# Two gates and the first weights of a convolution, taken step by step in another order

## The chip, the cores and the metric

The kernel runs on one core of one Trainium2 chip. A core has TensorE (matrix products, in the profile PE, its weight loads PEld), VectorE (DVE), ScalarE (ACT), GpSimd (POOL) and SyncE (SP), whose queue starts the transfers from device memory. Each engine runs its own instructions strictly in the order of its own list; between engines there are semaphores. The metric is the device time of one execution in microseconds, and lower is better.

## The reference, cut to what matters

An encoder trunk of two layers runs over two sequences of 512 and 256 tokens (768 columns together), with 1024 features (eight blocks of 128 rows) in float32. Layer 0 mixes tokens by attention within a window, layer 1 by a gated convolution of width 3. After each mixer comes an MLP and then a gated embedding. The places that matter here are the gated embedding that ends layer 0 and the start of the convolution:

```
h = rms_norm(x, norm_ple[0])
x = x + (p[0] @ ple_w_proj[0]) * sigmoid(h @ ple_w_gate[0])
h = rms_norm(x, norm_mix[1])
b_gate, c_gate, u = split(h @ conv_w_in)
z = c_gate * u
```

## The kernel before, in words

Activations lie transposed: a block `x(m)` is 128 features by 768 tokens. Every float32 operand is split in two parts, a high part (`whi`, `zhi`, `vhi` for weights, `xs` and `t` for inputs) written by ScalarE and a low part (`wlo`, `zlo`, `vlo`), which is the operand less its high part, written by VectorE. A product takes high by high, high by low and low by high on TensorE. Weights arrive as `wraw`, 128x1024 each, in three buffers; a fourth fetch waits until the low part of the first has been taken.

`ple` computes the gated embedding for the eight blocks in the order 0, 4, 1, 5, 2, 6, 3, 7 (`PAIRED`). For one block TensorE makes the gate product (two banks of 384 columns). VectorE multiplies it by the reciprocal root `r` (`gt<-gate`, L1206, for the last block L1259), ScalarE takes the sigmoid (L1207, L1260), VectorE multiplies by the projected embedding `pr` and adds to `x` (L1208 and L1210, L1266 and L1267). Then the block is made ready for the next norm `n3` (`plain_block`): ScalarE writes `xs<-x` times the gain, VectorE its low part (L304 and L305 for the first four blocks, L309 and L310 for the others), ScalarE squares the block (L195, L1273) and VectorE adds the square to `acc` (L196, L1280).

The convolution's products, save the first, use a scheme of seven smaller products on halves of 384 columns. They need sums of blocks: ScalarE copies two blocks (`q`, L326), VectorE makes four sums (`t13`, L345 and L346, and `t42`, L350 and L351), and ScalarE and VectorE split the two results (`high`, L355, and `low`, L361). The weights need sums as well (`sums32`, L409 and L410; `sums14`, L414 and L415), and their parts are split at L434 (high) and L445 (low), in groups called direct, second, s32, s14 and w22.

`conv_weights(0, 0, True)`, named `c`, is the first pair of weight arrays of the convolution. It is used as it comes, in 96 matmuls (`plain`, L1499: 48 for output `c1` with `zhi` and `zlo`, 48 for `c2` with `whi` and `wlo`, the last group of six of each 48 being that of block 7). `conv_weights(1, 0)`, named `v`, is the second pair, for the first of the eleven products of seven (`seven`). Between them stands the norm: `acc` is split into `ah` and `al` (L83, L84), four matmuls with ones give the sum of squares `ss` (L235), and `rstd_steps` makes the reciprocal root of it in three steps. `logs` is `v<-ss` on VectorE (L252), and `ln<-ss`, an exponential and a square on ScalarE (L254, L255, L256); `newton` is L260 and `result` L267 on VectorE. The logarithm needs another table than the sigmoid, and `table()` loads it (L216). `squares` then squares the root into `r2` on ScalarE (L1510), and `first(0)`, `first(1)` multiply `c1` and `c2` by it (L1516).

Inside `seven` these steps wait in a list, `pend`, and `late(n)` takes the next `n` at fixed places. For the first product of seven all four single banks `a`, `c`, `b` and `d` are of tag A. It runs as twelve matmuls each, L466: `a` (w11), then the copy `c<-a` (L1533), `b` (s3), `a` again (s2), the copy `d<-a` (L1547), `c` (w12), `a` (s1), `d` (w22), `a` (s4). `low<-a,p` (L1472) must have read `a` after s1 before s4 writes it again.

The order of ScalarE, TensorE and VectorE in this stretch is the order in which the code is written, since it stands in `tc.manual_schedule` blocks. The transfers' order on SyncE follows from the scheduler.

Of the kernel before, what the change touches and what calls it, by code (L numbers as in the profile page):

```python
# [13 lines left out]
AF = mybir.ActivationFunctionType  # L14
ALU = mybir.AluOpType
# [5 lines left out]
KB = D // P  # L21
SEQS = (512, 256)
T = sum(SEQS)
# [24 lines left out]
def trunk_kernel(ctx: ExitStack, tc: tile.TileContext, a: dict, out: bass.AP):  # L48
    nc = tc.nc
    act, dve, pe = nc.scalar, nc.vector, nc.tensor  # L50
# [13 lines left out]
    def gain(i, m):  # L64
        return vec[:, i * KB + m : i * KB + m + 1]
# [26 lines left out]
    def weight(src, n, raw=None, tag="w"):  # L92

        m = CH if src is None else src.shape[1]
        if raw is None:
            raw = fetch(src)
        pool, bufs = (wp, 2) if tag == "w" else (more, 1)
        hi, lo = (pool.tile([P, CH], F32R, tag=f"{tag}{p}", name=f"{tag}{p}", bufs=bufs) for p in ("hi", "lo"))
        split(hi[:, :m], lo[:, :m], raw[:, :m])
        return blocks(hi[:, :m], n), blocks(lo[:, :m], n)  # L100
# [15 lines left out]
    def both(name="mm", tag=None):  # L116

        return [t[:, :H] for t in fresh(name, 2, tag)]
# [29 lines left out]
    def slot(i, name, dt=F32R, n=T):  # L148

        return (slots if i < 32 else more).tile([P, n], dt, tag=f"S{i}", name=name)  # L150

    def big(name, dt=F32):

        nonlocal turn
        if more is None:
            return tmp.tile([P, T], dt, tag="t", name=name)
        turn += 1
        return tmp.tile([P, T], dt, tag=f"q{turn % 6}", name=name, bufs=1)
# [12 lines left out]
    class Norm:  # L171
# [9 lines left out]
        def block(self, m, xb):  # L181
            g = gain(self.i, m)
            hi, lo = (slot(self.places[8 * p + m], f"xs_{self.name}") for p in range(2))
            self.xs[0].append(hi[:])
            self.xs[1].append(lo[:])
            act.activation(hi[:], xb, AF.Copy, scale=g)
            dve.scalar_tensor_tensor(lo[:], xb, g, hi[:].bitcast(F32), ALU.mult, ALU.subtract)
            self.square(m, xb)
# [91 lines left out]
    class Norm7(Norm):  # L280
# [9 lines left out]
        def place(self):  # L290
            return slot(self.free.pop(0), "xs7")
# [40 lines left out]
    class Sums:  # L332
# [30 lines left out]
        def steps(self):  # L363
            return [
                self.t13,
                lambda: self.high(0),
                self.t42,
                lambda: self.high(1),
                lambda: self.low(0),
                lambda: self.low(1),  # L370
            ]
# [97 lines left out]
    pj = [dram.tile([KB, P, T], F32, name=f"pj{l}") for l in range(2)]  # L469
# [353 lines left out]
    def x(m, o=0, n=T):  # L823
        return pairs[m // 2][:, m % 2, o : o + n]
# [8 lines left out]
    PAIRED = [m + i for m in range(KB // 2) for i in (0, KB // 2)]  # L833
# [356 lines left out]
    def gate(w, xs, o, n):  # L1190
        ts = terms_of(w, [[t[:, o : o + n] for t in p] for p in xs])
        if n == T:
            gp = both("gate")
            group2(gp, ts)
            return pieces(gp)
        gp = fresh("gate")
        group(gp, ts, n)
        return [(gp[:, :n], 0, n)]

    def gated(l, m, gp, r, o, n, nxt, places):  # L1200

        pr = places(m) if callable(places) else slot(places[m % 3], "pr", F32)
        nc.sync.dma_start(pr[:, :n], pj[l][m, :, o : o + n])
        t = big("gt")
        for ps, i, e in gp:
            dve.tensor_tensor(t[:, i:e], ps, r[:, o + i : o + e], ALU.mult)  # L1206
        nxt.gated = act.activation(t[:, :n], t[:, :n], AF.Sigmoid).ins  # L1207
        dve.tensor_tensor(t[:, :n], pr[:, :n], t[:, :n], ALU.mult)  # L1208
        xb = x(m, o, n)
        dve.tensor_tensor(xb, xb, t[:, :n], ALU.add)  # L1210
        return xb

    def ple(norm, nxt):

        def place(m):
            return more.tile([P, CH], F32, tag=("sum0", "sum1", "zhi")[PAIRED.index(m) % 3], name="pr", bufs=1)

        def product(m, w):
            return gate(w, norm.xs, 0, T)

        def weights(i):
            return weight(a["gate"][0, PAIRED[i]], KB)

        def block(i, gp):
            m = PAIRED[i]
            nxt.block(m, gated(0, m, gp, r, 0, T, nxt, place))

        r = None
        for i in range(5):
            gp = product(PAIRED[i], weights(i))  # L1230
            r = norm.rstd(psum) if r is None else r
            block(i, gp)
            if i in (1, 3):
                weave(nxt.combine(i // 2))
        gp = product(PAIRED[5], weights(5))
        with tc.manual_schedule(engines={ET.Activation, ET.PE, ET.DVE}):
            w6 = weights(6)
            block(5, gp)
            w7 = weights(7)
            g6 = product(PAIRED[6], w6)  # L1240
            c = conv_weights(0, 0, True)
            sums = nxt.copied(2, 6)
            sums.t13()
            sums.t42()
            g7 = product(PAIRED[7], w7)
            block(6, g6)
            c.split("direct")
            sums.high(0)
            sums.high(1)
            sums.low(0)  # L1250
            sums.low(1)
            c.high("second")
            v = conv_weights(1, 0)
            m = KB - 1
            pr = place(m)
            nc.sync.dma_start(pr[:, :T], pj[0][m])
            t = big("gt")
            for ps, o, e in g7:
                dve.tensor_tensor(t[:, o:e], ps, r[:, o:e], ALU.mult)  # L1259
            nxt.gated = act.activation(t[:], t[:], AF.Sigmoid).ins  # L1260
            nxt.last = nxt.gated
            nxt.table()
            c.low("second")
            sq = big("sq")
            nxt.copied(m - KB // 2)
            dve.tensor_tensor(t[:], pr[:, :T], t[:], ALU.mult)  # L1266
            dve.tensor_tensor(x(m), x(m), t[:], ALU.add)  # L1267
            nxt.plain_block(m, x(m))
            sums = nxt.copied(m)
            v.sums32()  # L1270
            sums.t13()
            sums.high(0)
            act.activation(sq[:], x(m), AF.Square)  # L1273
            v.high("direct")
            sums.t42()
            v.low("direct")
            sums.high(1)
            sums.low(0)
            sums.low(1)
            dve.tensor_tensor(nxt.acc, nxt.acc, sq[:], ALU.add)  # L1280
            v.high("s32")
            parts = nxt.acc_parts()
            v.sums14()
            v.low("s32")
        return c, v, parts

    def last_ple(norm, full, rest, prs, ys, finals):
# [107 lines left out]
    def conv_weights(kind, p, plain=False):  # L1395
        f = (KB, 2 * KB, 0)[kind] + p
        return Weights7(a["w_in"][f], a["w_in"][f + KB // 2], plain)

    def mixer_conv(norm, w, v, norm_parts, held, finals, places, outs):
# [11 lines left out]
        pend, after, kept, done = [], [], {}, {}  # L1411
# [77 lines left out]
        def plain(w):  # L1489

            ps = [both(f"c{i + 1}", "BC"[i]) for i in range(2)]
            for i in range(2):
                for k in range(KB):
                    m, h = PAIRED[k] % (KB // 2), PAIRED[k] // (KB // 2)
                    c = slice(P * m, P * m + P)
                    hi, lo = w.w[f"w{i + 1}{h + 1}"]
                    for j, (wt, part) in enumerate(((hi, 0), (hi, 1), (lo, 0))):
                        for o in range(2):
                            pe.matmul(  # L1499
                                ps[i][o],  # L1500
                                lhsT=wt[:, c],
                                rhs=xs[f"x{h + 1}{1 + o}"][m][part],
                                start=k == 0 and j == 0,
                                stop=k == KB - 1 and j == 2,
                            )
            logs, newton, result = norm.rstd_steps(psum, norm.sum_squares(psum, parts=norm_parts, tag="A"))

            def squares():
                result()
                act.activation(r2[:], norm.r, AF.Square)  # L1510

            def first(i):
                kept["c", i] = big(f"c{i + 1}")
                for o in range(2):
                    c = slice(H * o, H * o + H)
                    dve.scalar_tensor_tensor(  # L1516
                        kept["c", i][:, c], ps[i][o], 1.0 - 2 * i, r2[:, c], ALU.mult, ALU.mult
                    )

            pend.extend([logs, newton, squares, lambda: first(0), lambda: first(1)])  # L1520

        a_out = a["w_out"]

# [89 lines left out]
    behind, product, w0 = second_inputs(xs0[24:])  # L1613
    w = [weight(a["w_o0"][2], 4)] * 2
    w2 = weight(a["w_o2"], 2, tag="z")
    for i, m in enumerate(PAIRED):
        if i == 1:
            w += [weight(a["w_o0"][3], 4)] * 2
        ps = both()
# [103 lines left out]
```

## Time and profile before

| what | value |
|---|---|
| time, median of 3 runs | 1702.33 us (1701.73 to 1704.52) |
| time of the profiled execution | 1702.36 us |
| its span, first to last instruction | 1700.6 us |
| TensorE busy over the span | 97% |
| VectorE, ScalarE busy | 83%, 53% |
| TensorE busy in 865 to 906 us | 36.27 of 41.00 us |
| TensorE busy in 906 to 1060 us | 153.69 of 154.00 us |

Times in the profile are microseconds from the start of the span. A row of the timeline gives the start, the length, the engine, the line, the operation with its output and inputs, the shape, how many like it were merged, and in brackets how long the engine had sat idle before it and for whose result. One engine's next instruction can start before the one ahead has ended, so the distance between starts is shorter than an instruction's length.

### The profile page before, as it was taken

To read this page: it belongs to the slowest core of one execution; us is meant where nothing else is said; L and a number is where in the kernel's file an instruction comes from. 1 tells how busy PE (TensorE), PEld (TensorE's weight loads), DVE (VectorE), ACT (ScalarE), POOL (GpSimd) and SP (SyncE) were. 2 spreads that over 40 slices of the span, in tenths; PEclk is the share of its full clock that TensorE was granted. 3 is DMA by queue.
4 is the path that set the end of the run, shared out by engine and by line. 5 is a ranking of instruction groups with operands and counts; after the bars stand their busy time and mean duration, and the time that the engine had idled before them with its cause. 6 is when DMAs were issued, how large, how long until landed. Compare 5 with 4: busy or idle time off the path is not lost.

```text
span 1700.6 us, 24086 instructions
## 1 busy us (share of the span) xinstructions
PE 1653.7 (97%) x9410; PEld 1592.2 (94%) x9410; DVE 1415.1 (83%) x2304; ACT 907.5 (53%) x1451; POOL 1.0 (0%) x12
## 2 busy tenths in 40 slices
PE   8999999989999999999999999999999999999996
PEld 7887788989999999999999999999999999999986
DVE  6588888889999989987888877858999999998776
ACT  6367756754455455544654334545445445554544
POOL 0000000000000000000000000000000000000000
PEclk9999999999999999999999999999999999999998
DMA  8654322211122211221212212211122211222222
GB/s 262 193 135 121 106 81 81 87 50 67 71 76 74 74 70 68 74 99 66 100 60 75 74 63 76 76 61 50 62 75 74 74 67 72 75 74 86 82 76 93
DMA packets 47843, 144.58 MB, mean 85 GB/s; under 512 B 6081, under 2 KB 10689, under 8 KB 47729
## 3 DMA queue, kind: packets, MB, share of 16 engines
q1 hardware_dynamic: 45168, 139.89, 24.2%
q10 hardware_dynamic: 2560, 3.15, 0.7%
q8 instruction: 74, 1.21, 0.3%
q14 instruction: 41, 0.33, 0.1%
HBM read 123.10 MB, written 10.48 MB: 79 GB/s over the span
## 4 chain that ended last, share of the span: by engine, by line
PE 59%; DVE 29%; ACT 8%; issue 3%; DMA 0%; DVEq 0%; ACTq 0%; SPq 0%
PE a L466 17%; PE mm L129 9%; PE mm L138 8%; PE b L466 4%; PE gate L138 4%; PE B L466 3%; PE C L466 3%; DVE t L361 3%; DVE wlo L445 3%; DVE y L938 3%; DVE zlo L445 2%; DVE act L394 1%; PE d L466 1%; ACT y L941 1%; DVE sum L410 1%
## 5 line engine op out<-in xcount | busy, mean ns | idle before, releaser
L434 ACT ACTIVATE whi<-sum 128x1024 fp32r<-128x1024 f32 x67 | 70.5, 1052 | 146.9 <-PE a L466 146.9
L941 ACT ACTIVATE y<-y 128x768 f32<-128x768 f32 x64 | 53.7, 840 | 144.6 <-DVE y L938 144.5
L466 PE MATMUL a<-xs,whi 128*128 128x384 f32 x624 | 123.4, 340 | 4.2 <-ACT whi L434 3.4
L466 PEld LDWEIGHTS a<-xs,whi 128*128 128x128 f32 x624 | 111.2, 189 | 4.9 <-ACT whi L434 3.7
L466 PE MATMUL a<-t,zhi 128*128 128x384 f32 x536 | 109.9, 338 | 3.4 <-ACT c L1054 3.1
L466 PE MATMUL b<-t,zhi 128*128 128x384 f32 x536 | 109.4, 338 | 0.5 <-ACT ln L254 0.5
L466 PE MATMUL a<-t,whi 128*128 128x384 f32 x536 | 108.8, 336 | 0.9 <-ACT d L1547 0.9
L466 PEld LDWEIGHTS a<-t,zhi 128*128 128x128 f32 x536 | 94.9, 188 | 4.3 <-ACT c L1054 3.8
L466 PE MATMUL a<-act,whi 128*128 128x384 f32 x448 | 96.5, 337 | 0.0
L466 PEld LDWEIGHTS b<-t,zhi 128*128 128x128 f32 x536 | 95.4, 189 | 0.9 <-ACT ln L254 0.9
L466 PEld LDWEIGHTS a<-t,whi 128*128 128x128 f32 x536 | 94.8, 188 | 1.2 <-ACT d L1547 1.2
L445 DVE TENSOR_TENSOR wlo<-wraw,whi 128x1024 fp32r<-128x1024 f32 x72 | 87.7, 1217 | 6.8 <-ACT whi L434 6.8
L445 DVE TENSOR_TENSOR wlo<-sum,whi 128x1024 fp32r<-128x1024 f32 x67 | 81.9, 1222 | 10.2 <-ACT whi L434 10.2
L1110 DVE TENSOR_TENSOR x<-x,a 128x384 f32<-128x384 f32 x112 | 60.7, 552 | 33.9 <-PE a L466 33.6
L434 ACT ACTIVATE zhi<-sum 128x1024 fp32r<-128x1024 f32 x67 | 71.0, 1060 | 22.3 <-DVE sum L410 22.2
L138 PE MATMUL mm<-xs_mix,whi 128*128 128x512 f32 (+1 forms) x320 | 82.9, 342 | 0.0
L434 ACT ACTIVATE whi<-wraw 128x1024 fp32r<-128x1024 f32 x72 | 75.7, 1052 | 11.6 <-PE C L466 6.1
L445 DVE TENSOR_TENSOR zlo<-sum,zhi 128x1024 fp32r<-128x1024 f32 x67 | 81.6, 1217 | 0.0
L466 PEld LDWEIGHTS a<-act,whi 128*128 128x128 f32 x448 | 79.9, 188 | 0.0
L355 ACT ACTIVATE t<-y 128x768 fp32r<-128x768 f32 x56 | 47.1, 842 | 41.2 <-DVE y L346 30.7
L83 ACT ACTIVATE whi<-wraw 128x1024 fp32r<-128x1024 f32 (+2 forms) x49 | 50.0, 1019 | 34.4 <-PE mm L129 13.9
L466 PE MATMUL a<-xs,wlo 128*128 128x384 f32 x312 | 67.7, 339 | 0.1
(316 smaller groups left out, 4488.0 us busy)
## 6 DMA issues: line engine op xcount, KB each, us to landing
wraw<-in_up SPq DMA_DIRECT2D x64, 512.0 KB, 3.5
wraw<-in_down SPq DMA_DIRECT2D x64, 512.0 KB, 3.5
wraw<-in_w_in SPq DMA_DIRECT2D x24, 512.0 KB, 3.5
wraw<-in_gate SPq DMA_DIRECT2D x16, 512.0 KB, 3.5
pj<-pjs SPq DMA_DIRECT2D x16, 384.0 KB, 3.3
wraw<-in_w_q SPq DMA_DIRECT2D x8, 512.0 KB, 4.8
wraw<-in_w_out SPq DMA_DIRECT2D x8, 512.0 KB, 3.5
x_in<-in_x SPq DMA_DIRECT2D x8, 384.0 KB, 7.6
```

Source lines behind the costliest of these rows:

```text
L83: first = act.activation(hi, src, AF.Copy)
L129: pe.matmul(t, lhsT=w, rhs=x[:, o:e], start=first and i == 0 and j == 0, stop=last and i == n - 1 and j == 2)
L138: pe.matmul(ps[:, o:e], lhsT=w, rhs=x[:, o:e], start=i == 0 and j == 0, stop=i == n - 1 and j == 2,)
L355: act.activation(t[0][:], (self.q1, self.q2)[i][:], AF.Copy)
L361: dve.tensor_tensor(lo[:], (self.q1, self.q2)[i][:], hi[:].bitcast(F32), ALU.subtract)
L394: dve.tensor_tensor(lo[:], self.q2[:], hi[:].bitcast(F32), ALU.subtract)
L434: act.activation(hi[:], src, AF.Copy)
L445: dve.tensor_tensor(lo[:], src, hi[:].bitcast(F32), ALU.subtract)
L466: pe.matmul(ps, lhsT=a, rhs=b, start=start and i == 0, stop=i == len(terms) - 1, skip_group_check=True)
L938: dve.scalar_tensor_tensor(t[:, o:e], src, 0.0, r[:, o:e], op, ALU.mult)
L941: act.activation(t[:], t[:], AF.Square)
L1110: dve.tensor_tensor(t[:, o : o + H], t[:, o : o + H], f, op)
```

## The change

The helper `block` of `ple` becomes `steps`, which gives the four steps of a gate apart: `times`, `sigmoid`, `added` and the making ready of the block. For the first six gates they are called one after the other as before. For the last two, blocks 3 and 7, the splits of the weights `c` and `v` and of the sums are written in between. The table load goes behind the square of block 7, the low part of s32 ahead of `al`, and in the convolution the square of the root (`r2`) goes from one step of `pend` to the next one, behind the copy `d<-a`. No instruction is added or taken away on any of the engines.

```
-            block(5, gp)
+            for step in steps(5, gp):
+                step()
             w7 = weights(7)
-            g6 = product(PAIRED[6], w6)
+            gp = product(PAIRED[6], w6)
             c = conv_weights(0, 0, True)
             sums = nxt.copied(2, 6)
             sums.t13()
             sums.t42()
-            g7 = product(PAIRED[7], w7)
-            block(6, g6)
-            c.split("direct")
+            times, sigmoid, added, block = steps(6, gp)
+            gp = product(PAIRED[7], w7)
+            c.high("direct")
+            times()
+            c.low("direct")
+            sigmoid()
+            c.high("second")
+            added()
+            c.low("second")
             sums.high(0)
+            block()
+            sums.high(1)
+            v = conv_weights(1, 0)
+            times, sigmoid, added, block = steps(7, gp)
+            m = KB - 1
+            sums.low(0)
+            nxt.copied(m - KB // 2)
+            times()
+            sigmoid()
+            sums.low(1)
+            v.sums32()
+            added()
+            nxt.plain_block(m, x(m))
+            sums = nxt.copied(m)
+            v.high("direct")
+            v.low("direct")
+            sums.t13()
+            sums.high(0)
+            v.high("s32")
+            sums.t42()
             sums.high(1)
             sums.low(0)
             sums.low(1)
-            c.high("second")
...
+            sq = big("sq")
+            act.activation(sq[:], x(m), AF.Square)
             nxt.last = nxt.gated
             nxt.table()
...
             dve.tensor_tensor(nxt.acc, nxt.acc, sq[:], ALU.add)
-            v.high("s32")
+            v.low("s32")
             parts = nxt.acc_parts()
             v.sums14()
-            v.low("s32")
...
             def squares():
-                result()
                 act.activation(r2[:], norm.r, AF.Square)
+                first(0)
...
-            pend.extend([logs, newton, squares, lambda: first(0), lambda: first(1)])
+            pend.extend([logs, newton, result, squares, lambda: first(1)])
```

ScalarE's list from the copies of blocks 2 and 6 (`q`, the first row) to the last sigmoid, before:

```order
L326 ACTIVATE q<-x,vec 128x768 x2
L1207 ACTIVATE gt<-gt 128x768
L304 ACTIVATE xs_8878<-x,vec 128x384
L304 ACTIVATE x_8879<-x,vec 128x384
L195 ACTIVATE sq<-x 128x768
L434 ACTIVATE zhi<-wraw 128x1024
L355 ACTIVATE t_8891<-q 128x768
L355 ACTIVATE t_8894<-q 128x768
L434 ACTIVATE whi<-wraw 128x1024
L1260 ACTIVATE gt<-gt 128x768
L216 ACT_TABLE_LOAD
```

The same stretch now:

```order
L326 ACTIVATE q<-x,vec 128x768 x2
L434 ACTIVATE zhi<-wraw 128x1024
L1235 ACTIVATE gt<-gt 128x768
L434 ACTIVATE whi<-wraw 128x1024
L355 ACTIVATE t_8886<-q 128x768
L304 ACTIVATE xs_8889<-x,vec 128x384
L304 ACTIVATE x_8890<-x,vec 128x384
L195 ACTIVATE sq<-x 128x768
L355 ACTIVATE t_8898<-q 128x768
L326 ACTIVATE q<-x,vec 128x768
L1235 ACTIVATE gt<-gt 128x768
```

The high part `zhi` of the convolution's first weights now stands ahead of the sigmoid of block 3, `whi` right behind it, and the table load has left this stretch.

VectorE's list from the product's multiplication by `r` for block 7 (`gt<-gate`) to the low part of that block's input (`xs_8922`), before:

```order
L1259 TENSOR_TENSOR gt<-gate,rstd_ple_8336 128x384 x2
L445 TENSOR_TENSOR wlo<-wraw,whi 128x1024
L1266 TENSOR_TENSOR gt<-pr,gt 128x768
L1267 TENSOR_TENSOR x<-x,gt 128x768
L310 SCALAR_TENSOR_TENSOR xs_8922<-x,vec,xs_8921 128x768
L409 TENSOR_TENSOR sum<-wraw 128x512
L410 TENSOR_TENSOR sum<-sum,wraw 128x512
```

And now:

```order
L1232 TENSOR_TENSOR gt<-gate,rstd_ple_8336 128x384 x2
L361 TENSOR_TENSOR t_8899<-q,t_8898 128x768
L409 TENSOR_TENSOR sum<-wraw 128x512
L410 TENSOR_TENSOR sum<-sum,wraw 128x512
L1238 TENSOR_TENSOR gt<-pr,gt 128x768
L1239 TENSOR_TENSOR x<-x,gt 128x768
L310 SCALAR_TENSOR_TENSOR xs_8922<-x,vec,xs_8921 128x768
L445 TENSOR_TENSOR wlo<-wraw,whi 128x1024
```

The sums of the second pair of weights moved ahead of the last addition to `x`, and `wlo` of the first pair has gone to the gate of block 3; the `wlo` that ends the second list is that of the second pair.

ScalarE's list from the copies of block 7 to the first part of the norm's sum (`ah`), as one piece of the difference:

```order
 L326 ACTIVATE q<-x,vec 128x768
-L355 ACTIVATE t_8931<-q 128x768
-L1273 ACTIVATE sq<-x 128x768
-L434 ACTIVATE whi<-wraw 128x1024
+L434 ACTIVATE whi<-wraw 128x1024
+L355 ACTIVATE t_8933<-q 128x768
+L434 ACTIVATE zhi<-sum 128x1024
 L355 ACTIVATE t_8941<-q 128x768
-L434 ACTIVATE zhi<-sum 128x1024
+L1296 ACTIVATE sq<-x 128x768
+L216 ACT_TABLE_LOAD
 L83 ACTIVATE ah<-acc_mix_8258 128x768
```

The square of block 7 and the table load now stand last ahead of `ah`.

More of the change, by code (lines that the diff above doesn't have):

```diff
@@ L1222, in weights, with steps, times, sigmoid @@
             return weight(a["gate"][0, PAIRED[i]], KB)
-        def block(i, gp):
+        def steps(i, gp):
             m = PAIRED[i]
-            nxt.block(m, gated(0, m, gp, r, 0, T, nxt, place))
+            pr = place(m)
+            nc.sync.dma_start(pr[:, :T], pj[0][m])
+            t = big("gt")
+            def times():
+                for ps, o, e in gp:
+                    dve.tensor_tensor(t[:, o:e], ps, r[:, o:e], ALU.mult)
+            def sigmoid():
+                nxt.gated = act.activation(t[:], t[:], AF.Sigmoid).ins
+            def added():
+                dve.tensor_tensor(t[:], pr[:, :T], t[:], ALU.mult)
+                dve.tensor_tensor(x(m), x(m), t[:], ALU.add)
+            return times, sigmoid, added, lambda: nxt.block(m, x(m))
         r = None
@@ L1231, in ple @@
             r = norm.rstd(psum) if r is None else r
-            block(i, gp)
+            for step in steps(i, gp):
+                step()
             if i in (1, 3):
@@ L1237, in ple @@
             w6 = weights(6)
-            block(5, gp)
+            for step in steps(5, gp):
+                step()
             w7 = weights(7)
-            g6 = product(PAIRED[6], w6)
+            gp = product(PAIRED[6], w6)
             c = conv_weights(0, 0, True)
@@ L1251, in ple @@
             sums.low(1)
-            c.high("second")
[L1253 to L1260, printed above, removed]
+            sq = big("sq")
+            act.activation(sq[:], x(m), AF.Square)
             nxt.last = nxt.gated
             nxt.table()
[L1263 to L1279, printed above, removed]
             dve.tensor_tensor(nxt.acc, nxt.acc, sq[:], ALU.add)
-            v.high("s32")
+            v.low("s32")
             parts = nxt.acc_parts()
             v.sums14()
-            v.low("s32")
         return c, v, parts
```

## The prediction, on record before the changed kernel ran

> **What bounds the kernel now.** First the page's span, then the waits of TensorE from 800 to 925 us, then its timeline around the change, then the stage windows. The waits:
>
> ```profile
> span 1700.6 us, 24086 instructions
> ...
> PE c L1499 <- ACT zhi L434: 1.1, 1, 1.1
> PE a L466 <- ACT d L1547: 0.9, 1, 0.9
> PE ss L235 <- DVE al L84: 0.5, 1, 0.5
> PE b L466 <- ACT ln L254: 0.5, 1, 0.5
> ...
> PE c L1499 <- DVE xs L310: 0.4, 1, 0.4
> ...
> ```
>
> The reader is to see that TensorE's waits of this stretch lie at the seam between the last gate and the convolution's first products, and behind both other engines: new weights (`zhi`), the last block (`xs`), the norm's sum (`al`), its logarithm (`ln`) and a copy (`d`). Next TensorE's rows there:
>
> ```profile
> 872.60 0.52 PE L129 MATMUL gate<-xs_ple,wlo 128*128 128x384 f32 x2
> ...
> 883.98 0.33 PE L1499 MATMUL c<-xs,whi 128*128 128x384 f32 x1
> ...
> 891.97 0.51 PE L1499 MATMUL c<-xs,wlo 128*128 128x384 f32 x2
> ...
> 894.62 1.56 PE L466 MATMUL a<-xs,whi 128*128 128x384 f32 x8
> ...
> 905.42 1.66 PE L466 MATMUL a<-t,whi 128*128 128x384 f32 x8 [0.92 <-ACT d L1547]
> ...
> 909.72 1.57 PE L466 MATMUL a<-xs,whi 128*128 128x384 f32 x8
> ```
>
> From 883.98 to 891.97 stand 46 starts without a wait, so a matmul costs 7.99/46 = 0.174 us. The gate's last two start at 872.60, so the convolution is due at 872.95. Up to 905.42 stand 96 + 4 + 4x12 = 148 matmuls, 25.7 us, but 32.47 pass: 6.75 us are lost, and 0.1 more behind the last wait, since the distance after a wait is longer (8 matmuls in 1.66 there, 1.57 at 909.72). So 6.9 us is all that can be had. What is won stays won if nothing new waits later:
>
> ```profile
> 906.00:1060.00 154.00, 153.69 (x877) 152.74 (x876) 122.06 (x173) 59.35 (x82) 0.00 (x0) 1.00 0.19 70
> ```
>
> TensorE (first pair) is busy 153.69 of 154.00 there, VectorE (third) 122.06, so VectorE has room to follow an earlier TensorE.
>
> **The change part by part.** Nothing is added or removed; the sum is over starts. I walk the new lists with the old durations and the old distances between starts. The clock is that of the old trace, and nothing ahead of 865.4 moves.
>
> ```profile
> 863.64 1.75 ACT L326 ACTIVATE q<-x,vec 128x768 f32<-128x768 f32 x2
> 868.39 0.85 ACT L1207 ACTIVATE gt<-gt 128x768 f32<-128x768 f32 x1 [3.00 <-DVE gt L1206]
> ...
> 878.95 1.28 ACT L216 ACT_TABLE_LOAD   x1
> 880.24 0.94 ACT L326 ACTIVATE q<-x,vec 128x768 f32<-128x768 f32 x1
> ...
> 886.43 0.83 ACT L1273 ACTIVATE sq<-x 128x768 f32<-128x768 f32 x1
> 887.17 1.04 ACT L434 ACTIVATE whi<-wraw 128x1024 fp32r<-128x1024 f32 x1
> 888.11 0.83 ACT L355 ACTIVATE t<-q 128x768 fp32r<-128x768 f32 x1
> ```
>
> ```profile
> 867.35 1.01 DVE L1206 TENSOR_TENSOR gt<-gate,rstd_ple 128x384 f32<-128x384 f32 x2
> ...
> 875.30 1.82 DVE L361 TENSOR_TENSOR t<-q,t 128x768 fp32r<-128x768 f32 x2
> 877.03 1.01 DVE L1259 TENSOR_TENSOR gt<-gate,rstd_ple 128x384 f32<-128x384 f32 x2
> 877.97 1.21 DVE L445 TENSOR_TENSOR wlo<-wraw,whi 128x1024 fp32r<-128x1024 f32 x1
> 879.10 0.95 DVE L1266 TENSOR_TENSOR gt<-pr,gt 128x768 f32<-128x768 f32 x1
> 880.08 0.96 DVE L1267 TENSOR_TENSOR x<-x,gt 128x768 f32<-128x768 f32 x1
> 882.11 1.02 DVE L310 SCALAR_TENSOR_TENSOR xs<-x,vec,xs 128x768 fp32r<-128x768 f32 x1 [1.06 <-ACT xs L309]
> 883.04 0.69 DVE L409 TENSOR_TENSOR sum<-wraw 128x512 f32<-128x512 f32 x1
> ...
> 884.37 0.55 DVE L345 TENSOR_TENSOR q<-q 128x384 f32<-128x384 f32 x1
> ```
>
> Distances on VectorE: 0.94 for two of 384 columns (877.03 to 877.97), 1.14 for 1024, 0.87 for 768 (1.73/2), 0.98 where the next needs the result (879.10 to 880.08), 1.33 for the pair of `sums32` (883.04 to 884.37). On ScalarE: 0.74 for 768 columns (886.43 to 887.17), 0.84 with a gain, 0.95 for 1024 (887.17 to 888.11).
>
> Step 1, `zhi` first. ScalarE sat idle 3.00 us ahead of block 3's sigmoid; `zhi` (1.04) fits in from 865.3. `zlo` then starts on VectorE at 867.35 + 0.94 = 868.29 and ends at 869.5, over 3 us before TensorE wants it. The waits for `zhi` and `zlo` go: TensorE starts the convolution at 872.95. The price is on the addition for block 3: 868.29 + 1.14 = 869.43 instead of at the sigmoid's end (868.39 + 0.85 = 869.24), 0.2 late, and nobody waits for it, as block 3's part is due only after 36 matmuls (879.2) and is there by 873.6. That TensorE carries four new waits for it I bound by 0 and, if each broke the pipeline, 0.4; the four waits are long over, so 0.
>
> Step 2, to block 7's gate. Multiplication 869.43, addition 870.42, `wlo` 871.29, the two halves of the low part 872.43 and 872.96, `acc` 873.49, `low(0)` of the sums 874.36, so `gt<-gate` of block 7 at 875.23 instead of 877.03. Of these 1.80 us, `low(1)` and `sums32` now standing between (0.87 + 1.33, against 1.13 for `wlo` before) take back 1.07: the multiplication by `pr` comes at 875.23 + 0.94 + 2.20 = 878.37 instead of 879.10, a gain of 0.73. `xs` ends at 881.36 and its low part at 882.41. TensorE, now earlier, wants them at 872.95 + 42 x 0.174 = 880.25: it loses 1.2 + 0.1 and 0.6 + 0.1, 2.0 together, and starts `c2` at 883.27, only 0.71 ahead.
>
> `sums32` needs the second array of the second pair. Its fetch waits for `zlo` and so goes out at 869.5 (875.4 before); the need is at 877.04, and VectorE's whole queue stands behind it. The landings of line L89, the weights' fetch, between 840 and 900 us (least, median, most):
>
> ```profile
> DMA to landing us min/median/max: 3.4/3.5/4.4
> ```
>
> Landed by 873.9 at this stage's slowest, it is in time by 3 us; cost 0 (its rival is below).
>
> Step 3, the norm.
>
> ```profile
> 892.98 0.96 DVE L84 TENSOR_TENSOR al<-acc_mix,ah 128x768 fp32r<-128x768 f32 x1 [0.91 <-ACT ah L83]
> 893.86 0.68 DVE L414 TENSOR_TENSOR sum<-wraw 128x512 f32<-128x512 f32 x1
> ...
> 895.06 1.22 DVE L445 TENSOR_TENSOR zlo<-sum,zhi 128x1024 fp32r<-128x1024 f32 x1
> 896.20 1.01 DVE L252 TENSOR_SCALAR v<-ss 128x384 f32<-128x384 f32 x2
> ```
>
> Behind the low part (start 881.39), VectorE waits till `whi` of the second pair is ready at 883.15 (ScalarE: `xs` 880.42, `q` 881.26, `whi` 882.10), takes `wlo` at 883.18 and the four sums 884.32 to 886.72. ScalarE: `high(0)` 885.63, `zhi` of s32 886.37, `high(1)` 887.32, square 888.05, table 888.90 to 890.18. VectorE: lows at 886.63 and 888.18, `acc` 889.05 to 890.00, `zlo` of s32 889.92 to 891.06. `ah` starts at 890.20 behind the table (0.16 later than `acc` alone would let it), ends at 891.04, `al` at 891.07: 1.91 earlier than 892.98. Then `zlo` (1.14) no longer stands between `al` and `v`: `v` at 891.07 + 0.88 + 1.20 = 893.15, 3.05 earlier than 896.20. TensorE is through `c2` at 883.27 + 8.34 = 891.6, does not wait for `ah`, waits for `al` (end 892.03) 0.3 + 0.1, and begins `a` at 892.71 instead of 894.62.
>
> The Trainium skill, page "ScalarE: Activation LUTs", section "What ACT_TABLE_LOAD costs", speaks against this part: it puts a drain of about 1380 ns on top of 1283 ns for each switch. This case's trace agrees with the first part alone: the load took 1.28 us and the next row starts 0.01 behind its end (878.95, 880.24), with no drain to be seen; what the page's figure would make of the sum stands with rival (b).
>
> Step 4, the first product of seven.
>
> ```profile
> 896.78 1.05 ACT L254 ACTIVATE ln<-ss,eps 128x384 f32<-128x384 f32 x2 [3.83 <-DVE v L252]
> ...
> 899.50 0.47 ACT L1533 ACTIVATE c<-a 128x384 f32<-128x384 f32 x1
> ...
> 904.14 0.84 ACT L1510 ACTIVATE rstd<-rstd_mix 128x768 f32<-128x768 f32 x1 [2.30 <-DVE rstd_mix L267]
> 904.89 0.47 ACT L1547 ACTIVATE d<-a 128x384 f32<-128x384 f32 x1
> ```
>
> `ln` follows the first `v`, so the whole chain `ln`, exponential, square, `c<-a` is 3.05 earlier. `b` is due at 892.71 + 2.09 = 894.80 and the first `ln` ends near 894.3: that wait goes. The next `a` is due at 896.89 and `c<-a` ends at 899.97 - 3.05 = 896.92: 0.2 with the restart. `d<-a` no longer stands behind `r2`; the s1 product needs it at 896.97 + 0.1 + 24 x 0.174 = 901.27, and it ends at 899.9. So that wait goes too, and TensorE is 4.15 us ahead. But VectorE is not:
>
> ```profile
> 908.82 0.55 DVE L1472 TENSOR_TENSOR low<-a,p 128x384 f32<-128x384 f32 x1
> ```
>
> Its chain root, `r2`, `first`, `z`, `low` runs unbroken from `v` and is 3.05 ahead, so `low` ends at 909.37 - 3.05 = 906.32, and the last `a` product, due at 901.27 + 4.17 = 905.45, must wait for it until 906.37, 0.9 + 0.1. This is the stall that takes the place of the one removed.
>
> The sum of TensorE's new losses: 2.0 + 0.4 + 0.2 + 1.0 = 3.6 against 6.9, a gain of 3.2 us: 1702.36 - 3.2 = **1699.1 us**, 0.19% under the median 1702.33, from which the profiled execution differs by 0.03. From there on both are bound to TensorE as before, and the gain is carried to the end.
>
> The bounds: each start is a sum of ten to twenty distances good to some 0.02, and three things end within 0.2 us at `al`; I give the sum 0.8 either way, 1698.3 to 1699.9.
>
> **The rivals.** (a) VectorE's chain comes out 0.9 faster, and the last `a` does not wait: TensorE then keeps 4.25 us, 1698.1. That would be so if `ln` did not wait for `v`: `ss` is complete some 0.6 us ahead of `v`. Against it, the row of `ln` shows just that wait, 3.83 us, ending 0.03 behind the first `v`, and neither has changed places.
>
> (b) The table load costs more at its new place, where it is exposed behind the square. With `ah` later by x, `al` is later by x, and the gain 3.2 less x. For it: behind the old load stood no row that somebody waited for. Against it: the next row came 0.01 behind it, which puts x at 0. Were the load to hold ScalarE twice its 1.28 us, x would be 1.3 and the time 1700.4. By the drain on the page of the Trainium skill named above, x would be 1.4 and the time, an estimate, 1700.5.
>
> (c) The gain dies behind the seam, because VectorE falls behind TensorE in the next products: 1702.4, no change. For it: VectorE is the later one by 1 us at the last `a`. Against it: it is busy 79% of the stage that follows.
>
> (d) Slower. The new place of `sums32` makes all of VectorE wait for a transfer. From a landing 7.5 us after the issue on, each further us delays block 7 by one, and the whole norm's chain with it; from 10.7 us on the kernel is slower. The run's longest landing of such a fetch:
>
> ```profile
> DMA to landing us min/median/max: 2.7/3.5/12.1
> ```
>
> With 12.1 it lands at 881.6, 4.6 late: a loss of 1.4, 1703.8. Against it stands 4.4 as the longest here.
>
> **How the numbers follow.** Forecast 0.67 (1699.1), (a) 0.13, (b) 0.08, (c) 0.05, (d) 0.07. A measurement of this kernel tells 0.2%, 3.4 us, from no change; that line is 1698.93, 0.2 below the forecast. So the forecast splits, about 0.4 of it faster and 0.6 the same: faster 0.27 + 0.13 = 0.40; slower (d), 0.06 once its mild part is left out; the same 0.54. The range reaches from 1697.6, (a) with the spread of the sum, to 1701.0, which takes in (b).
>
> **What would show it.** The first matmul of L1517 right behind the last gate's; waits for `xs` of about 1 and for its low part of about 0.5; none for `ah`, `ln` or `d`; a new one, about 0.8, of the `a` product that follows `d`, behind DVE `low`; and `ah` starting right at the table's end. A wait on L409 for a transfer, an `ah` over 0.5 us behind the table, or TensorE waits after 910 that were not there would make the prediction wrong.

## The result, and the profile after

The changed kernel takes 1697.8 us (median of 8 runs, 1696.68 to 1702.05) against 1702.36 (8 runs, 1701.4 to 1704.52) for the kernel before: a ratio of 0.9975, interval 0.9964 to 0.9986. Measured again later beside other runs it took 1699.16 (11 runs) against 1702.52 (15 runs): 0.9979, interval 0.997 to 0.9988. So it is faster by 0.25 or 0.21%, a hair past the 0.2% that the prediction drew as its line, with that line inside both intervals. The profiled execution took 1697.29, its span 1695.6.

First the waits of TensorE from 800 to 925 us, changed kernel (columns: us in total, times, longest):

```profile
PE c L1517 <- ACT xs L309: 0.9, 1, 0.9
PE a L466 <- DVE low L1490: 0.7, 1, 0.7
PE c L1517 <- DVE xs L310: 0.4, 1, 0.4
PE gate L129 <- DVE wlo L84: 0.3, 1, 0.3
```

The waits for `zhi`, `zlo`, `ah`, `al`, `ln` and `d` are gone. In their place stand the first row (the last block comes too late for the earlier TensorE) and the second, a wait that the kernel before didn't have. The `wlo` row is the gate's own and was there before. Next TensorE's timeline of the same execution:

```profile
871.06 0.52 PE L129 MATMUL gate<-xs_ple,wlo 128*128 128x384 f32 x2
871.42 0.33 PE L1517 MATMUL c<-xs,zhi 128*128 128x384 f32 x1
...
879.81 0.61 PE L1517 MATMUL c<-xs,zhi 128*128 128x384 f32 x2 [0.94 <-ACT xs L309]
...
880.87 0.62 PE L1517 MATMUL c<-xs,zhi 128*128 128x384 f32 x2 [0.44 <-DVE xs L310]
...
881.68 0.34 PE L1517 MATMUL c<-xs,whi 128*128 128x384 f32 x1
...
890.09 0.34 PE L235 MATMUL ss<-ah,ones 128*128 128x384 f32 x1
890.42 0.44 PE L235 MATMUL ss<-al,ones 128*128 128x384 f32 x1
890.70 0.34 PE L235 MATMUL ss<-ah,ones 128*128 128x384 f32 x1
...
893.14 1.56 PE L466 MATMUL b<-t,zhi 128*128 128x384 f32 x8
...
895.31 1.68 PE L466 MATMUL a<-t,zhi 128*128 128x384 f32 x8
896.83 0.86 PE L466 MATMUL a<-t,zlo 128*128 128x384 f32 x4
...
903.12 0.86 PE L466 MATMUL d<-t,vlo 128*128 128x384 f32 x4
904.71 1.66 PE L466 MATMUL a<-xs,whi 128*128 128x384 f32 x8 [0.72 <-DVE low L1490]
906.21 0.86 PE L466 MATMUL a<-xs,wlo 128*128 128x384 f32 x4
```

The convolution's first matmul now follows 0.36 us behind the start of the gate's last two: no gap. Those two matmuls start at 871.06 here and at 872.60 in the trace of before, 1.54 us apart, though nothing that they wait for was moved. So times of one trace can't be set against those of another. From here on two distances are used, measured the same way in every profile:

- **the way to the seam**: from the start of the span to VectorE's `wlo<-wraw,whi` of the last gate. It lies wholly in unchanged work.
- **the seam**: from that start to the first matmul of `b` in the second product of seven (`b<-t,zhi`).

VectorE's row for the start of the seam, before and then after:

```profile
863.89 1.22 DVE L84 TENSOR_TENSOR wlo<-wraw,whi 128x1024 fp32r<-128x1024 f32 x1
```

```profile
862.35 1.22 DVE L84 TENSOR_TENSOR wlo<-wraw,whi 128x1024 fp32r<-128x1024 f32 x1
```

And TensorE's row for its end, before and then after:

```profile
913.92 1.56 PE L466 MATMUL b<-t,zhi 128*128 128x384 f32 x8
```

```profile
909.00 1.56 PE L466 MATMUL b<-t,zhi 128*128 128x384 f32 x8
```

The seam took 913.92 - 863.89 = 50.03 us before and 909.00 - 862.35 = 46.65 after: 3.38 us gained, where the prediction worked out 3.2. The stage behind the seam, changed kernel (length, then pairs of busy us and instructions for PE, PEld, DVE, ACT, POOL, then granted clock, DMA share, GB/s):

```profile
906.00:1060.00 154.00, 153.62 (x874) 151.98 (x873) 121.57 (x170) 61.15 (x84) 0.00 (x0) 1.00 0.22 76
```

The granted clock is full, and TensorE is as busy there (153.62) as before (153.69).

### The profile page after: what moved, and what is told of

It reads as the page before. It is cut to its first block, busy times and chain, and to the rows that moved or that the text cites. A ratio compares the mean times of both kernels' runs of the same rounds, so it can differ in the third digit from the quotient of the medians.

```text
span 1695.6 us, 24086 instructions
## 1 busy us (share of the span) xinstructions
PE 1651.5 (97%) x9410; PEld 1590.6 (94%) x9410; DVE 1414.4 (83%) x2304; ACT 907.3 (54%) x1451; POOL 1.0 (0%) x12
## 4 chain that ended last, share of the span: by engine, by line
PE 59%; DVE 29%; ACT 8%; issue 3%; DMA 0%; DVEq 0%; ACTq 0%; SPq 0%
PE a L466 18%; PE mm L129 9%; PE mm L138 9%; PE b L466 4%; PE B L466 3%; PE C L466 3%; DVE t L361 3%; DVE wlo L445 3%; DVE y L938 3%; PE gate L138 3%; DVE zlo L445 2%; DVE act L394 1%; PE c L466 1%; ACT y L941 1%; PE d L466 1%
```

## The experiments

Ten kernels ran. The table has one profile of each, and a second one of the kernel before and of the changed kernel. All distances start at the seam's start: "first ys" ends at the start of TensorE's first row of the projection that follows the convolution (`mm<-ys`), "last ys" at the start of its last row.

| kernel | way to the seam | seam | first ys | last ys | span |
|---|---|---|---|---|---|
| before | 863.89 | 50.03 | 195.77 | 262.58 | 1700.6 |
| before, again | 861.63 | 50.03 | 195.76 | 262.57 | 1698.8 |
| changed | 862.35 | 46.65 | 192.37 | 259.54 | 1695.6 |
| changed, again | 866.07 | 46.65 | 192.40 | 259.64 | 1700.2 |
| zhi_alone (from before) | 861.36 | 48.93 | 194.68 | 261.50 | 1697.5 |
| square_alone (from before) | 864.63 | 49.84 | 195.57 | 262.43 | 1702.7 |
| square_early (from changed) | 866.0 | 46.88 | 192.62 | 259.80 | 1699.5 |
| s32low_late (from changed) | 861.36 | 47.78 | 193.51 | 260.68 | 1697.5 |
| table_early (from changed) | 863.96 | 46.62 | 192.36 | 259.54 | 1697.1 |
| sums32_late (from changed) | 861.56 | 45.95 | 191.69 | 258.85 | 1694.4 |
| wlo_behind_low (from changed) | 862.76 | 45.63 | 192.06 | 259.23 | 1695.7 |
| norm_early (from changed) | 862.33 | 43.80 | 190.23 | 257.06 | 1693.3 |

**Both kernels again.** No edit. Expected of the changed kernel, and of the one before:

> The changed kernel once more. The seam is measured from the start of the last gate's low part of the weights on VectorE (L84, 863.89 in the old trace) to the start of the second product of seven's product b on TensorE (913.92): 50.0 us before. Theory: the change is worth what the seam loses, 3.4 us in the changed trace, so the seam is again 46.6 us here within 0.1, and the time 1699 within 1. Rival: the 4.6 us between the medians belong to the change, and parts of the program far from the seam are shorter too: then the 1.5 us that the changed profile was ahead by when it reached the seam would be there again, whatever the start of the run did.

> The kernel before, unchanged, for a second profile. Theory: the seam is 50.0 us again within 0.1, and the way from the start of the span to the seam differs from the first profile's 863.89 by about 1 us, as the changed kernel's did (862.35), since the order up to there is the same in both. Rival: the way up to the seam is 863.9 again within 0.2, so that the 1.5 us would be the change's.

The seam came out as 46.65 and 50.03, both times to 0.01 us of the first profiles, while the way to it was 866.07 and 861.63: this time the changed kernel was the later one there, by 4.4 us. The way moved by 3.7 and 2.3 us from one profile of a kernel to the other, more than the 1 us expected. So the seam repeats and the total does not. One execution's time can't tell a gain of 3 us, while one profile of the seam does. The gap between the first medians, 4.6 us, is more than the seam's gain, the later 3.4 about as much; each interval (2.4 to 6.1 us, 2.0 to 5.1 us) holds what the seam gives.

**Step 1 alone (zhi_alone).** The kernel before, with only the weights' parts moved:

```diff
...
             g7 = product(PAIRED[7], w7)
-            block(6, g6)
-            c.split("direct")
+            c.high("direct")
+            for ps, o, e in g6:
+                dve.tensor_tensor(t[:, o:e], ps, r[:, o:e], ALU.mult)
+            c.low("direct")
+            nxt.gated = act.activation(t[:], t[:], AF.Sigmoid).ins
+            dve.tensor_tensor(t[:], pr[:, :T], t[:], ALU.mult)
+            dve.tensor_tensor(x(m), x(m), t[:], ALU.add)
+            nxt.block(m, x(m))
```

> The kernel before with the first part of the change alone: the high part of the convolution's first weights ahead of block 3's sigmoid, its low part ahead of the multiplication by pr; all else as before. Theory: TensorE starts the convolution 1.8 us earlier but then waits for block 7, which comes only 1.1 us earlier (the low part zlo, 1.14, no longer stands ahead of block 7's gate), so the seam is 48.9 us (50.03 before, 46.65 with the whole change) and a wait for xs stands in place of the wait for zhi. Rival: this part carries the change, and the seam is 48.2 or less.

Measured 48.93, a gain of 1.10. TensorE's waits from 862 us on, this kernel:

```profile
PE a L466 <- ACT d L1557: 0.9, 1, 0.9
PE c L1509 <- ACT xs L309: 0.6, 1, 0.6
...
```

The waits for `zhi` and `zlo`, 1.1 and 0.3 before, are away, but one for the last block's `xs` has come up. Two thirds of the change's gain therefore needs the other steps. Removing a wait in front of TensorE is worth only the distance to what is late next.

**The norm's square (square_early and square_alone).** The changed kernel with the square ahead of copy `d` again, and the kernel before with the square alone moved behind it:

```diff
             def squares():
+                result()
                 act.activation(r2[:], norm.r, AF.Square)
-                first(0)
...
-            pend.extend([logs, newton, result, squares, lambda: first(1)])
+            pend.extend([logs, newton, squares, lambda: first(0), lambda: first(1)])
```

> The changed kernel with the convolution's list of steps as before: the square of the root again in the step ahead of the copy d. Theory: the wait for d comes back (about 1.0 us), but the wait for low that follows (0.7) goes, since TensorE is then no longer ahead of VectorE; the seam is 46.7 us, 0.1 longer than with the whole change. Rival: this part is worth its own wait, and the seam is 47.6 to 47.8.

> The kernel before with the last part of the change alone: the square of the root one step later, behind the copy d. Theory: the wait for d (0.9, 1.2 with the tail and the restart) goes, and TensorE stops instead at the last a for low, which VectorE reaches no sooner; the seam is 49.8 to 49.9 us against 50.03. Rival: the wait was worth what it lasted, and the seam is 48.9.

Measured 46.88 and 49.84: the move is worth 0.23 at the changed seam, where 0.1 was expected and the rival had 1.0 or more, and 0.19 at the old one. Each profile shows why it is so little. square_early has the one wait, square_alone the other:

```profile
PE a L466 <- ACT d L1565: 0.9, 1, 0.9
```

```profile
PE a L466 <- DVE low L1472: 0.7, 1, 0.7
```

A wait of 0.9 was exchanged for one of 0.7, two products of 12 matmuls later. The theory that VectorE's chain down to `low` sets this end stands; that the 0.9 us could be won by itself falls.

**The low part of the second weights (s32low_late).**

```diff
-            v.low("s32")
             parts = nxt.acc_parts()
             v.sums14()
+            v.low("s32")
```

> The changed kernel with the low part of s32 behind the sums of s14 again, between al and v. Theory: v, and with it the whole chain to low, is 1.14 us later; the waits for ln (0.5) and for the copy c come back, and the seam is 47.8 us. Rival: the low part only changes places with work that is hidden anyway, and the seam stays 46.6.

Measured 47.78, so this move is worth 1.13. TensorE again has a wait for the logarithm (and one of 0.2 for the copy `c`), and the one for `low` keeps its size:

```profile
...
PE a L466 <- DVE low L1490: 0.7, 1, 0.7
PE b L466 <- ACT ln L254: 0.5, 1, 0.5
...
```

With `zlo` between `al` and `v` the chain `v`, `ln`, `c`, root, `low` starts 1.1 us later, and all of that reaches TensorE. This is the term of step 3 on its own.

**The table load (table_early).** The load stands right behind the last sigmoid, where ScalarE had idle time:

```diff
             sigmoid()
+            nxt.last = nxt.gated
+            nxt.table()
...
-            nxt.last = nxt.gated
-            nxt.table()
```

> The changed kernel with the table load right behind the last sigmoid, where ScalarE sits idle 3.3 us, instead of behind the square. Theory: the load costs 1.28 us where it stands, acc ends within 0.2 of it, and al waits for VectorE's low part of s32 anyway, so the seam stays 46.6. Rival: a load that waits for the pipe to empty costs over 1 us more in the chain, and the seam is 45.6 or less.

Measured 46.62 against 46.65. ScalarE's rows, first the changed kernel, then table_early:

```profile
886.38 0.83 ACT L1296 ACTIVATE sq<-x 128x768 f32<-128x768 f32 x1
887.23 1.28 ACT L216 ACT_TABLE_LOAD   x1
888.53 0.85 ACT L83 ACTIVATE ah<-acc_mix 128x768 fp32r<-128x768 f32 x1
```

```profile
889.98 0.85 ACT L83 ACTIVATE ah<-acc_mix 128x768 fp32r<-128x768 f32 x1 [1.16 <-DVE acc_mix L1299]
```

In the changed kernel the load begins 0.02 behind the square's end, takes 1.28 and lets `ah` start 0.02 behind its own. In table_early `ah` waits 1.16 for VectorE's sum instead, so behind the square the load only fills time in which ScalarE would have waited anyway. From the square's end to `ah` it is 1.32 us in all. The drain of about 1380 ns that the Trainium skill (page "ScalarE: Activation LUTs", section "What ACT_TABLE_LOAD costs") adds to each switch didn't appear at this place.

**The sums of the second pair (sums32_late).**

```diff
             sums.low(1)
-            v.sums32()
             added()
             nxt.plain_block(m, x(m))
             sums = nxt.copied(m)
+            v.sums32()
```

> The changed kernel with sums32 behind block 7's low part instead of ahead of its multiplication by pr. Theory: block 7 comes 1.3 us earlier, the wait for xs (0.9) goes, and the norm's chain is 0.8 earlier, since the two sums now fill the wait for whi of the second pair: seam 45.9 us. Rival: TensorE's loss ahead of c2 is made up at al, and the seam stays 46.6.

Measured 45.95, 0.70 better than the change itself. Its waits:

```profile
PE a L466 <- DVE low L1490: 0.7, 1, 0.7
PE ss L235 <- DVE al L84: 0.6, 1, 0.6
...
```

The 0.9 for `xs` is gone, since 1.33 us of VectorE no longer stand ahead of the last block, and 0.6 for `al` is there instead: of the 1.3 us that block 7 came earlier about half is lost again at `al`, which the rival had for all of it. So the place that the change gave to `sums32` costs it 0.7 net.

**VectorE's weight part behind `low` (wlo_behind_low).** In the first product of seven alone:

```diff
-                v.split("direct")
+                v.split("direct") if not first else v.high("direct")
             product7(a, w, "s1", xs, False)
             low(kind, p, a, q, H)
             if v:
+                v.low("direct")
                 v.sums14()
```

> The changed kernel with the low part of the third pair's direct group (wlo, 1.14) behind low instead of ahead of it in the first product of seven. Theory: the new wait for low (0.7, about 0.8 to 0.9 with the restart) goes and nothing waits in its place: seam 45.7 us. Rival: the low part comes too late for the next product, which waits for it instead, and the seam stays 46.6.

The seam came out at 45.63, 1.02 better: in VectorE's list `wlo` (1.22 us) stood right ahead of `low`, and that was the new wait. But at the first `ys` only 192.37 - 192.06 = 0.31 of it is left. TensorE's rows behind the seam's end, this kernel:

```profile
919.22 1.68 PE L466 MATMUL a<-xs,whi 128*128 128x384 f32 x8 [0.18 <-DVE low L1490]
...
925.41 0.97 PE L466 MATMUL b<-t,zlo 128*128 128x384 f32 x4 [0.32 <-DVE zlo L445]
```

The first of these waits, in the second product of seven, is new. The second, in the third product, is only longer than it was: the list of TensorE's weight loads (PEld) has it in the kernel before and in the changed kernel too, both times as in the row below, while in this kernel it is 0.6:

```profile
PEld b L466 <- DVE zlo L445: 0.4, 1, 0.4
```

Why the gain fades shows in VectorE's row for `low` of the second product, changed kernel and then this one:

```profile
918.54 0.55 DVE L1490 TENSOR_TENSOR low<-a,p 128x384 f32<-128x384 f32 x1
```

```profile
918.62 0.55 DVE L1490 TENSOR_TENSOR low<-a,p 128x384 f32<-128x384 f32 x1
```

From the seam's start that is 56.19 and 55.86 us. The edit exchanges two places in VectorE's list and makes none of it shorter: TensorE comes 1.02 us earlier, VectorE only 0.33, and what VectorE gained is about what is left. So "nothing waits in its place" held inside the seam alone.

**All of it together (norm_early).** Block 7's gate ahead of the sums' low parts and of the addition of block 3's square, the table load behind the sigmoid, both squares added and the norm's parts (`ah`, `al`) formed ahead of the next weights' low parts, `sums32` behind block 7, and `wlo` behind `low` (that last piece is shown above):

```diff
             sums.high(0)
-            block()
+            m = PAIRED[6]
+            nxt.plain_block(m, x(m))
+            sq6 = big("sq")
+            act.activation(sq6[:], x(m), AF.Square)
             sums.high(1)
             v = conv_weights(1, 0)
             times, sigmoid, added, block = steps(7, gp)
             m = KB - 1
+            times()
+            nxt.copied(m - KB // 2)
+            sigmoid()
+            nxt.last = nxt.gated
+            nxt.table()
             sums.low(0)
-            nxt.copied(m - KB // 2)
-            times()
-            sigmoid()
+            added()
             sums.low(1)
+            nxt.plain_block(m, x(m))
+            sq = big("sq")
+            act.activation(sq[:], x(m), AF.Square)
+            dve.tensor_tensor(nxt.acc, nxt.acc, sq6[:], ALU.add)
+            dve.tensor_tensor(nxt.acc, nxt.acc, sq[:], ALU.add)
+            sums = nxt.copied(m)
             v.sums32()
-            added()
-            nxt.plain_block(m, x(m))
-            sums = nxt.copied(m)
             v.high("direct")
-            v.low("direct")
+            parts = nxt.acc_parts()
...
             sums.high(1)
+            v.low("direct")
             sums.low(0)
+            v.low("s32")
             sums.low(1)
-            sq = big("sq")
-            act.activation(sq[:], x(m), AF.Square)
-            nxt.last = nxt.gated
-            nxt.table()
-            dve.tensor_tensor(nxt.acc, nxt.acc, sq[:], ALU.add)
-            v.low("s32")
-            parts = nxt.acc_parts()
             v.sums14()
...
```

> A version made from the reasons: the changed kernel with block 7's gate ahead of block 3's square, the table load behind the last sigmoid, block 7's square, acc and ah ahead of the sums, sums32 behind block 7, and wlo behind low. Theory: all waits of TensorE at the seam go but small ones for c (0.1) and perhaps low; the seam is 43.8 us, 6.2 us shorter than before and 2.9 shorter than with the change, so 0.37% faster than before. Rival: VectorE, which has the same work in less time, is the bound before the sum of squares, and the seam stays over 45.

The seam took 43.80, 6.23 less than before. TensorE's waits from 862 to 940 us, without the gate's own `wlo`:

```profile
PE b L466 <- DVE zlo L445: 0.3, 1, 0.3
...
PE a L466 <- ACT c L1555: 0.3, 1, 0.3
PE a L466 <- DVE low L1494: 0.2, 1, 0.2
```

Of these only the wait for the copy `c` lies in the seam (0.3 where 0.1 was expected); `low` and `zlo` lie behind its end, at the two places of wlo_behind_low. At the first `ys` 5.54 is left: this kernel loses the same 0.69 there as wlo_behind_low does (6.23 to 5.54, and 4.40 to 3.71). In time: 1695.95 us (median of 5 runs, 1695.12 to 1697.56) against 1703.02 (9 runs), a ratio of 0.9965, interval 0.9951 to 0.9979. It is the fastest of the kernels here by its seam and by its distance to the last `ys`; its interval for the time overlaps that of the change.

## Why the prediction was right, point by point

The clock of the trace after is 1.54 us ahead of the prediction's, so 1.54 is added to its times here.

**What bounds the kernel** held: TensorE's waits at the seam made up what was to be had there, 6.9 us, and norm_early won 6.23 of them.

**Step 1** held to 0.02 us up to the addition for block 3. The rows of VectorE:

```profile
866.74 1.21 DVE L445 TENSOR_TENSOR zlo<-wraw,zhi 128x1024 fp32r<-128x1024 f32 x1
...
873.67 1.01 DVE L1232 TENSOR_TENSOR gt<-gate,rstd_ple 128x384 f32<-128x384 f32 x2
...
875.46 0.68 DVE L409 TENSOR_TENSOR sum<-wraw 128x512 f32<-128x512 f32 x1
...
876.79 0.95 DVE L1238 TENSOR_TENSOR gt<-pr,gt 128x768 f32<-128x768 f32 x1
...
879.79 1.02 DVE L310 SCALAR_TENSOR_TENSOR xs<-x,vec,xs 128x768 fp32r<-128x768 f32 x1 [1.06 <-ACT xs L309]
```

`zlo` starts at 868.28 on the prediction's clock (868.29 there).

**Step 2** held: block 7's product by `r` at 875.21 (875.23), that by `pr` at 878.33 (878.37), the low part of `xs` at 881.33 (881.39). TensorE's waits for the two, 0.94 and 0.44 in its list, brought `c2` to 883.22 (883.27): a loss of 1.9 for 2.0. L409 has no wait beside it, so rival (d), the transfer, did not come.

**Step 3** held in its order and was mis-sized by 0.14: the term for `al` was 0.4. TensorE's two `ss` rows start 0.33 apart and the next 0.28, against 0.174 for a matmul that waits for nothing, so the loss is 0.16 + 0.10 = 0.26. The sum had `ah` at 890.20 where it came at 890.07, and three ends were within 0.2 us of each other there.

```profile
889.41 0.96 DVE L84 TENSOR_TENSOR al<-acc_mix,ah 128x768 fp32r<-128x768 f32 x1
...
891.49 1.01 DVE L252 TENSOR_SCALAR v<-ss 128x384 f32<-128x384 f32 x2
```

`al` at 890.95 (891.07) and `v` at 893.03 (893.15) carry the same 0.12 on.

**Step 4** held. The wait for `ln` is gone. The copy `c` cost the 0.2 foreseen, though the list of TensorE's matmuls doesn't show it (that of its weight loads does, with 0.2): from `b` at 893.14 to the next `a` at 895.31 are 2.17 us where 12 matmuls take 2.09, and the next start follows after 1.52 instead of 1.39, 0.08 + 0.13 in all. The wait for `d` became one for `low`, 0.72 in the list; it starts at 904.71, where 903.12 + 4 x 0.174 = 903.82 was due, so 0.89, and 0.11 behind it: 1.0 as predicted.

```profile
902.97 1.22 DVE L445 TENSOR_TENSOR wlo<-wraw,whi 128x1024 fp32r<-128x1024 f32 x1
904.10 0.55 DVE L1490 TENSOR_TENSOR low<-a,p 128x384 f32<-128x384 f32 x1
```

The losses are then 1.9 + 0.26 + 0.21 + 1.0 = 3.4 instead of 3.6, and 6.85 less 3.4 is the 3.38 measured within 0.1.

**The rivals.** (a), TensorE keeping 4.25 because `low` isn't waited for, did not come: `ln` waited for `v`, as the prediction had held against it.

```profile
892.07 1.05 ACT L254 ACTIVATE ln<-ss,eps 128x384 f32<-128x384 f32 x2 [2.70 <-DVE v L252]
```

(b) fell: `ah` came 0.02 behind the load, and table_early took 46.62. (c) did not come for the change, and it doesn't begin at some size of gain: sums32_late is 4.08 ahead at the seam's end and still 4.08 at the first `ys`. It came in part in the two kernels with `wlo` behind `low`, an edit that moves TensorE ahead and VectorE hardly. So "VectorE has room to follow", taken from a busy share of 79%, holds for this change and not for every order; a busy share over 154 us doesn't tell which product of seven is tight.

**From there on the gain is "carried to the end"**: nearly. Of 3.38 in the seam, 195.77 - 192.37 = 3.40 is there at the first `ys` and 262.58 - 259.54 = 3.04 at the last. The 0.36 lost between is told of below. From the last `ys` to the end of the span it is 574.1 and 574.6 us in the two profiles of the kernel before, 573.7 and 574.5 in those of the changed one, so no loss shows there beyond this spread. The forecast of 3.2 lies between the two numbers.

**The chances.** The time, 1697.8 and then 1699.16, lies in the range both times, and its two medians stand on either side of the line of 1698.93 that the prediction drew by its 0.2%. A forecast this near the line couldn't do better than split its chance over both sides. The spread of the way to the seam, 4.7 us over the profiles here, wasn't in the prediction's bounds, which took the sum off one execution's 1702.36 as if only the sum were unsure. The range's lower end, 1697.6, is (a) less 0.5, not less the 0.8 given for the sum. That the first median lies 0.2 above this end is luck: the end was set for (a), which did not come.

## What to carry to other kernels

Where a stage starts and ends in repeatable rows, measure that distance rather than the total: it settled effects of 0.2 us in one profile each, in kernels whose total moves by 5 or 6 us between executions (1699.81 to 1704.87 and 1696.09 to 1702.22 in the larger sets). Price an edit at a seam by what is late next on each of the other engines, walked start to start with the distances of the old trace; a wait removed is worth only the way to the next one (1.10 for 1.4 us of listed waits in zhi_alone, 0.2 for 0.9 in the square's). And after a gain look at the next stages' weights and low parts: where the edit made TensorE earlier but not VectorE, only what VectorE gained was left soon behind (0.31 of 1.02 in wlo_behind_low); where both came earlier, all of it was (0.70 of 0.70 in sums32_late).

## What the runs showed of the hardware that was not expected

**The way to the seam scatters.** The same instructions reach the seam between 861.36 and 866.07 us in twelve profiles, with no order by kernel, while the seam itself repeats within 0.01 us for each of the two kernels profiled twice. Between the first two profiles the 1.54 us arose at about 15 us (0.87) and from 160 to 220 us, in the attention (the rest); why they arose is not known.

**A wait that the trace doesn't explain.** In the projection behind the convolution, VectorE sits idle 0.46 us, which the view puts down to ScalarE's `ys`. Rows of ScalarE, VectorE and TensorE of the changed kernel:

```profile
1055.37 3.05 ACT L83 ACTIVATE ys<-b 128x768 fp32r<-128x768 f32 x4
```

```profile
1056.47 0.95 DVE L84 TENSOR_TENSOR ys<-b,ys 128x768 fp32r<-128x768 f32 x1
1057.87 3.08 DVE L84 TENSOR_TENSOR ys<-b,ys 128x768 fp32r<-128x768 f32 x3 [0.46 <-ACT ys L83]
```

```profile
1058.29 1.22 PE L129 MATMUL mm<-ys,whi 128*128 128x384 f32 x4
```

And before:

```profile
1061.41 4.14 DVE L84 TENSOR_TENSOR ys<-b,ys 128x768 fp32r<-128x768 f32 x4
```

```profile
1063.22 0.88 PE L129 MATMUL mm<-ys,whi 128*128 128x384 f32 x4
```

By the distance of ScalarE's four rows its second `ys` ended near 1056.9, some 0.9 us before VectorE went on, so it was not this result that was missing. TensorE's four matmuls took 1.22 instead of 0.88. From the first to the last `ys` it is 67.16 to 67.24 us in the seven profiles that show this (both of the changed kernel, square_early, s32low_late, sums32_late, wlo_behind_low, table_early), and 66.81 to 66.86 in the five that don't (both of before, zhi_alone, square_alone, norm_early). So it goes by kernel, but not by the size of the gain: norm_early, with the largest, is free of it. VectorE's own order there is the same in all twelve, its separate waits on semaphores included. What differs is how much stands ahead of it: up to the first of the VectorE rows shown its list in the trace has 202 separate waits in each of the seven and 203 or 204 in the five, beside 1527 other entries in all. Whether that has to do with it was not tried, and the cause stays open.
